# High and low part of an activation side by side, and one 512-column product for both

## The chip, the cores and the metric

The kernel runs on one core of a Trainium2 chip. The metric is the device time of one execution in microseconds: the median of three timed runs. A profiled execution of the same program has its own time and a trace; the numbers that are worked out below come from that trace.

## The reference

A trunk of two layers over 256 tokens of width 1024, all in float32. Cut to what matters:

```python
def hybrid_mixer(x, ...):
    q, k, v, z, xbc, dt_raw, g_att, g_ssm = _split(x @ w_in, IN_SPLITS)
    att = moba_attention(rope(q), rope(k), v)            # 16 heads of 64
    y_ssm = mamba2_branch(z, xbc, dt_raw, ...)           # 32 heads of 64, width 2048
    merged = (sigmoid(g_att) * (att @ w_attn_proj)       # 1024 x 1024
              + sigmoid(g_ssm) * (y_ssm @ w_ssm_proj))   # 2048 x 1024
    return merged @ w_out

def reference(x, ...):
    for i in range(DEPTH):                               # 2 layers
        x = layer_norm(ALPHA * x + hybrid_mixer(x, ...))
        x = layer_norm(ALPHA * x + square(relu(x @ w_up)) @ w_down)   # 1024 -> 4096 -> 1024
    return x
```

## The kernel before

**Precision.** Every large product is made of three. A float32 operand is split into a high part, rounded to the chip's short float32 format (`fp32r`), and a low part, what the rounding left. The sum of high times high, high times low and low times high is accumulated in one bank of PSUM. The high part is a cast on ScalarE (ACT), the low part a subtraction on VectorE (DVE).

**Weights.** They come in halves of 128 x 1024 floats, 512 KB each, 185 a layer. SyncE's queue loads a half (`load_half`, L119), ACT casts it (`high_half`, L125), DVE subtracts (`low_half`, L133). `need(L, h, s)` says in which slot a half is used: its low part is issued four slots ahead, its high part six, its load fourteen.

**Order.** The whole kernel is one list of slots, 370 a layer. A slot holds the matmuls of about 1.4 us. `at(s, f)` hangs other work in front of slot s. In each slot the order is: high casts, low parts, hung steps, loads, the slot's matmuls; every engine runs what it gets in this order, and waits where its input isn't there. `res(s)` takes the next free slot for a step that has matmuls of its own.

**Two kinds of product.** `cols` and `rows` (through `mm3`, L143 to L145) keep 128 tokens as weights of the array and move 512 columns of the weight matrix. `gemm_ct` (L407 to L409) does it the other way: a 128 x 128 tile of the weight matrix is loaded, and the 256 tokens are moved, so that the output stands with channels on partitions. One slot of `gemm_ct` does four steps of 128 rows (k), three products of 256 columns each; two slots make 128 output channels over 1024 rows.

**Who uses gemm_ct.** The input projection's state space part (`acc_x`), its gates (`acc_z`, `acc_ga`, `acc_gs`) and the step sizes (`dtp`); then the three that are touched here: the attention projection (`acc_ap`, slots B+178 on, two 256-column outputs share a bank), the state space projection (`acc_sp`, slots B+194 on, 2048 rows, four slots per output) and the up projection of the MLP in chunks 1 to 7 of 512 channels (`up`, four outputs of 128 channels per chunk, two of them in a bank). Chunk 0 of up goes through `cols` and is transposed (`hTt`, `up_turn`). Within a period of 16 slots eight slots of up alternate with eight of the down projection (`acc_d`).

**Evacuation.** `ap_evac` multiplies a full bank by the attention gate on DVE (L849). `merge` multiplies by the other gate and adds (L857, L858), then `merge_high` and `merge_low` split the result for the output projection. In the MLP `up_relu` reads a bank on ACT (L910), `up_square` squares on DVE (L914), `up_high` and `up_low` split into `hT` for the down projection.

**Banks.** Eight banks of PSUM: four with the tag `acc`, two `yav`, two `tmp`. Up's outputs are in `yav`, transposes in `tmp`. **SBUF** for activations: x as two tiles xh and xl of 128 x 8 x 256, attT and yT as pairs of tiles (high, low) of 128 x 4 x 256 (`new_T`), from the same pool of 31 tiles as the weights.

Of the kernel before, what the change touches and what calls it, by code (L numbers as in the profile page):

```python
# [64 lines left out]
def trunk(ctx: ExitStack, tc: tile.TileContext, x, xT, pos, w, pch, hp, lnp, out):  # L65
# [172 lines left out]
    def new_x(name):  # L238
        return (sb.tile([128, KD, S], F32R, name=name + "h", tag="xh", bufs=1),
                sb.tile([128, KD, S], F32R, name=name + "l", tag="xl", bufs=1))  # L240
# [71 lines left out]
    def new_T(name):  # L312
        return (u_tile(name + "h", F32R, (128, 4, S)), u_tile(name + "l", F32R, (128, 4, S)))

# [68 lines left out]
    def plan_layer(L):  # L383
# [14 lines left out]
        def gemm_ct(o, h, half, src=None, k0=None, nh=1):  # L398

            wh, wl = W[L, h]  # L400
            src = src or xsrc
# [192 lines left out]
        def ct_bank(base, h0, c0, c1, name, src, nh=1):  # L594

            g = {}

            def slot(c, half):
                if c == c0 and half == 0:
                    g["o"] = new_acc(f"acc_{name}{L}_{c}")  # L600
                o = g["o"][:, (c - c0) * S:(c - c0) * S + S]
                gemm_ct(o, h0 + nh * c + half // 2, half % 2, src, 4 * half, nh)

            for c in range(c0, c1):
                for half in range(2 * nh):
                    s = base + 2 * nh * c + half
                    if half % 2 == 0:
                        need(L, h0 + nh * c + half // 2, s)
                    slots[s] = (slot, c, half)
            return g  # L610
# [9 lines left out]
        for d, name, base, h0, n, func in ((zs, "z", B + 114, 57, 4, AF.Silu), (ga, "ga", B + 146, 73, 2, AF.Sigmoid),  # L620
                                           (gs, "gs", B + 162, 81, 2, AF.Sigmoid)):
            for b in range(n):
                banks = [ct_bank(base, h0, 4 * b + 2 * j, 4 * b + 2 * j + 2, name, None) for j in range(2)]
                at(base + 8 * b + 8, act_evac, d, b, banks, func, name)
# [59 lines left out]
        def at_out(s, g):  # L684
            if g % 2 == 0:
                attT[g // 2] = new_T(f"attT{L}{g // 2}")
            r = slice(2 * (g % 2), 2 * (g % 2) + 2)
            split_psum(s, attT[g // 2][0][:, r, :], attT[g // 2][1][:, r, :], G.pop(("av", g)))
# [120 lines left out]
        def ss_high(g):  # L809
            if g % 2 == 0:  # L810
                yT[g // 2] = new_T(f"yT{L}{g // 2}")
            k = 2 * (g % 2)
            nc.scalar.copy(out=yT[g // 2][0][:, k:k + 2, :], in_=E["y", g])

        def ss_low(g):
            k = 2 * (g % 2)
            hi, lo = (a[:, k:k + 2, :] for a in yT[g // 2])
            nc.vector.tensor_tensor(out=lo, in0=E.pop(("y", g)), in1=hi.bitcast(F32), op=OP.subtract)
# [128 lines left out]
        for c in range(1, 8):  # L947
# [176 lines left out]
```

## Time and profile before

| | |
|---|---|
| timed, median of three | 1173.37 us |
| timed, lowest and highest | 1172.96 and 1173.97 us |
| the profiled execution, its own time | 1172.3 us |
| its span, from the first to the last instruction | 1170.6 us |
| granted TensorE clock over the span | 0.997 |
| TensorE matmul (PE), busy | 1150.9 us, 8160 products |
| VectorE (DVE), busy | 864.3 us |
| ScalarE (ACT), busy | 650.7 us |
| read from HBM | 208.93 MB, 179 GB/s |

PE is the matmul engine and PEld its loading of weights, which overlaps. A row of the timeline begins with the start and the duration; successive matmuls overlap, so the distance of two starts is less than a duration. In groups, the numbers behind the first bar are the busy time and the mean duration in ns; those behind the second are the engine's idle time ahead of these instructions and what ended it. In a list of waits the numbers are the total, how often, and the longest.

### The profile page before, as it was taken

The numbers are of one execution on the slowest core, as the hardware profiler recorded it, in microseconds if no ns is written. First come the engines' busy times: TensorE is split into PE (matmuls) and PEld (weight loads), VectorE is DVE, ScalarE is ACT, GpSimd is POOL, SyncE is SP. The second block draws the span as 40 slices with busy tenths as digits, with TensorE's granted clock in tenths as the row PEclk, the third lists the DMA queues.
The fourth block names the chain that finished last, engine by engine and source line by source line (L and its number), as shares of the span: only waits on it lengthen the run. The fifth ranks groups of instructions, "written<-read, shape, count | busy, mean of one in ns | idle before, by whom it ended". The sixth has DMA issues, their size and how long they took to land.

```text
span 1170.6 us, 20414 instructions
## 1 busy us (share of the span) xinstructions
PE 1150.9 (98%) x8160; PEld 1058.4 (90%) x8160; DVE 864.3 (74%) x1553; ACT 650.7 (56%) x927; POOL 54.9 (5%) x67
## 2 busy tenths in 40 slices
PE   6999999999999999999999999999999999999996
PEld 5999888999999899989889998889999998998995
DVE  4888987799865874564689888778987668556455
ACT  5665655888734363453456656568886353444341
POOL 1000000011110100000000000000111100000000
PEclk9999999999999999999999999999999999999998
DMA  9545564544466655557336455544445656555630
GB/s 343 189 144 181 193 181 159 180 137 137 163 210 216 241 185 194 187 196 248 132 104 218 146 180 190 193 155 170 134 150 181 219 214 215 199 181 192 204 126 36
DMA packets 61263, 211.37 MB, mean 181 GB/s; under 512 B 6993, under 2 KB 7345, under 8 KB 61169
## 3 DMA queue, kind: packets, MB, share of 16 engines
q1 hardware_dynamic: 59136, 204.04, 51.2%
q0 software_dynamic: 1744, 5.51, 1.5%
q8 instruction: 64, 1.05, 0.4%
q10 hardware_dynamic: 288, 0.52, 0.1%
q14 instruction: 31, 0.25, 0.1%
HBM read 208.93 MB, written 1.11 MB: 179 GB/s over the span
## 4 chain that ended last, share of the span: by engine, by line
PE 96%; DVE 2%; DMA 1%; SPq 0%; POOL 0%; issue 0%; POOLq 0%; ACT 0%
PE acc_x L407 5%; PE acc_x L409 5%; PE acc_x L408 5%; PE acc_d L143 5%; PE acc_d L145 5%; PE acc_d L144 5%; PE up L409 5%; PE up L408 5%; PE up L407 5%; PE acc_z L407 3%; PE acc_sp L409 3%; PE acc_sp L408 3%; PE acc_sp L407 3%; PE acc_z L408 3%; PE acc_z L409 3%; PE yp L748 2%
## 5 line engine op out<-in xcount | busy, mean ns | idle before, releaser
L133 DVE TENSOR_TENSOR wlo<-raw,whi 128x1024 fp32r<-128x1024 f32 (+1 forms) x371 | 443.8, 1217 | 27.1 <-ACT whi L125 12.5
L125 ACT CAST whi<-raw 128x1024 fp32r<-128x1024 f32 (+1 forms) x371 | 375.5, 1046 | 29.2 <-PE acc_ap L408 7.6
L505 DVE SCALAR_TENSOR_TENSOR cv<-acc_x,pc,cv 128x253 f32<-128x253 f32 (+2 forms) x192 | 92.4, 481 | 18.6 <-ACT cv L501 13.9
L914 DVE TENSOR_TENSOR rl<-rl 128x512 f32<-128x512 f32 x32 | 22.1, 691 | 110.5 <-ACT rl L910 110.3
L910 ACT ACTIVATE rl<-up 128x512 f32<-128x512 f32 x28 | 16.8, 599 | 153.8 <-PE up L409 134.0
L407 PE MATMUL acc_x<-x2h,whi 128*128 128x256 f32 x256 | 74.0, 289 | 0.0
L407 PE MATMUL acc_x<-x0h,whi 128*128 128x256 f32 x256 | 73.9, 289 | 0.0
L409 PE MATMUL acc_x<-x0h,wlo 128*128 128x256 f32 x256 | 72.4, 283 | 0.0
L409 PE MATMUL acc_x<-x2h,wlo 128*128 128x256 f32 x256 | 72.4, 283 | 0.0
L408 PE MATMUL acc_x<-x0l,whi 128*128 128x256 f32 x256 | 72.4, 283 | 0.0
L408 PE MATMUL acc_x<-x2l,whi 128*128 128x256 f32 x256 | 72.4, 283 | 0.0
L501 ACT ACTIVATE cv<-acc_x,pc 128x256 f32<-128x256 f32 x64 | 36.2, 566 | 62.1 <-PE acc_x L409 59.3
L407 PE MATMUL up<-x1h,whi 128*128 128x256 f32 x224 | 63.5, 284 | 0.0
L407 PE MATMUL up<-x3h,whi 128*128 128x256 f32 x224 | 63.5, 284 | 0.0
L409 PE MATMUL up<-x3h,wlo 128*128 128x256 f32 x224 | 63.4, 283 | 0.0
L409 PE MATMUL up<-x1h,wlo 128*128 128x256 f32 x224 | 63.4, 283 | 0.0
L408 PE MATMUL up<-x1l,whi 128*128 128x256 f32 x224 | 63.4, 283 | 0.0
L408 PE MATMUL up<-x3l,whi 128*128 128x256 f32 x224 | 63.4, 283 | 0.0
L332 POOL TENSOR_TENSOR rc<-rc,mhalf 128x8 f32<-128x8 f32 x16 | 32.0, 2002 | 612.1 <-DVE nm L656 445.0
L407 PEld LDWEIGHTS acc_x<-x0h,whi 128*128 128x128 f32 x256 | 49.0, 191 | 0.3 <-issue 0.2
L407 PEld LDWEIGHTS acc_x<-x2h,whi 128*128 128x128 f32 x256 | 49.0, 191 | 0.3 <-issue 0.2
L408 PEld LDWEIGHTS acc_x<-x0l,whi 128*128 128x128 f32 x256 | 49.1, 192 | 0.0
(749 smaller groups left out, 3511.9 us busy)
## 6 DMA issues: line engine op xcount, KB each, us to landing
raw<-in_w_dram SPq DMA_DIRECT2D x369, 512.0 KB, 3.8
pb<-csd SPq DMA_DIRECT2D x32, 256.0 KB, 3.9
ln<-in_lnp_dram POOLq DMA_DIRECT2D x16, 256.0 KB, 4.9
x_tok<-in_x_dram POOLq DMA_DIRECT2D x1, 1024.0 KB, 10.9
xraw<-in_xT_dram SPq DMA_DIRECT2D x3, 256.0 KB, 7.8
raw<-in_w_dram SPq DMA_DIRECT2D x2, 256.0 KB, 3.9
out_dram<-x_tok SPq DMA_DIRECT2D x2, 256.0 KB, 2.0
out_dram<-x_tok ACTq DMA_DIRECT2D x2, 256.0 KB, 2.0
```

Of the source, the lines that this page charges most:

```text
L125: nc.scalar.copy(out=hi[:, c], in_=raws[key][:, c])
L133: nc.vector.tensor_tensor(out=lo[:, c], in0=raw[:, c], in1=W[key][:, c].bitcast(F32), op=OP.subtract)
L143: nc.tensor.matmul(o, xh, wh, start=first, stop=False)
L144: nc.tensor.matmul(o, xh, wl, start=False, stop=False)
L145: nc.tensor.matmul(o, xl, wh, start=False, stop=last)
L332: nc.gpsimd.tensor_tensor(out=dst, in0=src, in1=mhalf[:, 0:n], op=OP.pow)
L407: nc.tensor.matmul(o, a, xh[:, kk, :], start=(k == 0), stop=False)
L408: nc.tensor.matmul(o, a, xl[:, kk, :], start=False, stop=False)
L409: nc.tensor.matmul(o, b, xh[:, kk, :], start=False, stop=(k == 8 * nh - 1))
L501: nc.scalar.activation(c, o, AF.Identity, scale=pc[:, q + 3:q + 4], bias=pc[:, q + 4:q + 5])
L505: nc.vector.scalar_tensor_tensor(out=c[:, d:S], in0=o[:, 0:S - d], scalar=pc[:, q + j:q + j + 1], in1=c[:, d:S], op0=OP.mult, op1=OP.add)
L748: nc.tensor.matmul(yp[64 * i:64 * i + 64, 128 * t:256], xt[:, t, hs], e[:, i, 256 * t:256 + 128 * t], start=(t == 0), stop=(t == 1))
```

## The change

Three projections (attention, state space, up chunks 1 to 7) get a new form of `gemm_ct`, `gemm_ct2`. High and low part of the activation lie next to each other, 256 columns each, and one product of 512 columns multiplies both by the high weights. Its left half is high times high, its right half high times low. The product with the low weights, 256 columns, is accumulated onto the left half. An output of 128 channels now fills a bank of 512 columns, and its halves must be added: ACT copies the right half to SBUF (`take_right`), DVE adds the left half to it (`add_left`).

- x (`new_x`) becomes one tile of 128 x 8 x 2 x 256; attT and yT (`new_T2`) become two tiles of 128 x 2 x 2 x 256 each.
- In up the outputs take `yav` and `tmp` banks in turn, one for each 128 channels. Relu on ACT and square on DVE are replaced by the copy and the add per output, and one DVE instruction (relu and square in one) for each 512 columns.
- In the attention projection each output has its own `acc` bank; the gate multiply goes from one per 512 columns to one per 256, behind the add.
- In the state space projection the copy and the add come ahead of the gate multiply; `merge`, `merge_high` and `merge_low` of all but the last output move one slot later.
- The other projections keep `gemm_ct`, with three products of 256 columns. No load, no weight and no cast of a weight is changed.

```diff
     def new_x(name):
-        return (sb.tile([128, KD, S], F32R, name=name + "h", tag="xh", bufs=1),
-                sb.tile([128, KD, S], F32R, name=name + "l", tag="xl", bufs=1))
+        both = sb.tile([128, KD, 2, S], F32R, name=name, tag="xhl", bufs=1)
+        return both[:, :, 0, :], both[:, :, 1, :], both
...
+    def new_T2(name):
+        return [u_tile(f"{name}{i}", F32R, (128, 2, 2, S)) for i in range(2)]
...
+        def gemm_ct2(o, h, half, src, k0=None, nh=1):
+            wh, wl = W[L, h]
             k0 = 4 * half if k0 is None else k0
             for i in range(4):
                 k, c = k0 + i, (4 * half + i) * 128
-                xh, xl, kk = src(k)
+                x2, kk = src(k)
                 a, b = wh[:, c:c + 128], wl[:, c:c + 128]
-                nc.tensor.matmul(o, a, xh[:, kk, :], start=(k == 0), stop=False)
-                nc.tensor.matmul(o, a, xl[:, kk, :], start=False, stop=False)
-                nc.tensor.matmul(o, b, xh[:, kk, :], start=False, stop=(k == 8 * nh - 1))
+                last = k == 8 * nh - 1
+                left = lambda: nc.tensor.matmul(o[:, 0:S], b, x2[:, kk, 0, :], start=False, stop=False)
+                if last:
+                    left()
+                nc.tensor.matmul(o, a, x2[:, kk].rearrange("p j s -> p (j s)"), start=(k == 0), stop=last)
+                if not last:
+                    left()
+
+        def take_right(out, o):
+            nc.scalar.copy(out=out, in_=o[:, S:2 * S])
+
+        def add_left(out, o):
+            nc.vector.tensor_tensor(out=out, in0=o[:, 0:S], in1=out, op=OP.add)
...
-        def ap_evac(c, g):
-            a = ga[c // 4][:, c % 4:c % 4 + 2, :].rearrange("p k s -> p (k s)")
-            nc.vector.tensor_tensor(out=a, in0=g["o"], in1=a, op=OP.mult)
-
-        for c in range(0, 8, 2):
-            g = ct_bank(B + 178, 89, c, c + 2, "ap", lambda k: (*attT[k // 4], k % 4))
-            at(B + 178 + 2 * c + 5, ap_evac, c, g)
+        T2 = {}
+
+        def right_aside(c, g, name):
+            T2[name, c] = sb.tile([128, S], F32, name=f"{name}s{L}{c}", tag="e15", bufs=4)
+            take_right(T2[name, c], g["o"])
+
+        def ap_gate(c, g):
+            a, t = ga[c // 4][:, c % 4, :], T2.pop(("ap", c))
+            add_left(t, g["o"])
+            nc.vector.tensor_tensor(out=a, in0=t, in1=a, op=OP.mult)
+
+        for c in range(8):
+            g = ct_whole(B + 178, 89, c, "ap", lambda k: (attT[k // 4][k % 4 // 2], k % 2))
+            at(B + 178 + 2 * c + 2, right_aside, c, g, "ap")
+            at(B + 178 + 2 * c + 3, ap_gate, c, g)
...
         def merge(c, g):
-            m = gs[c // 4][:, c % 4, :]
-            nc.vector.tensor_tensor(out=m, in0=g["o"][:, 0:S], in1=m, op=OP.mult)
+            m, t = gs[c // 4][:, c % 4, :], T2.pop(("sp", c))
+            add_left(t, g["o"])
+            nc.vector.tensor_tensor(out=m, in0=t, in1=m, op=OP.mult)
...
-            g = ct_bank(B + 194, 97, c, c + 1, "sp", lambda k: (*yT[k // 4], k % 4), nh=2)
+            g = ct_whole(B + 194, 97, c, "sp", lambda k: (yT[k // 4][k % 4 // 2], k % 2), nh=2)
             r = B + 194 + 4 * c + 4
-            at(r, merge, c, g)
-            at(r + (c < 7), merge_high, c)
-            at(r + (c < 7), merge_low, c)
+            at(r, right_aside, c, g, "sp")
+            at(r + (c < 7), merge, c, g)
+            at(r + 2 * (c < 7), merge_high, c)
+            at(r + 2 * (c < 7), merge_low, c)
...
         def up_slot(c, i, half):
-            if half == 0 and i % 2 == 0:
-                ub[c, i // 2] = new_yav(f"up{L}{c}{i}")
-            o = ub[c, i // 2][:, (i % 2) * S:(i % 2) * S + S]
-            gemm_ct(o, 125 + 8 * (c - 1) + i, half, msrc)
+            if half == 0:
+                ub[c, i] = (new_tmp if i % 2 else new_yav)(f"up{L}{c}{i}")
+            gemm_ct2(ub[c, i], 125 + 8 * (c - 1) + i, half, lambda k: (X[2 * L + 1][2], k))
+
+        def up_part(c, i):
+            return hr[c][:, i // 2, (i % 2) * S:(i % 2) * S + S]
+
+        def up_right(c, i):
+            if i == 0:
+                hr[c] = u_tile(f"rl{L}{c}")
+            take_right(up_part(c, i), ub[c, i])
+
+        def up_left(c, i):
+            add_left(up_part(c, i), ub.pop((c, i)))
+
+        def up_relu_square(c, j):
+            r = hr[c][:, j, :]
+            nc.vector.scalar_tensor_tensor(out=r, in0=r, scalar=0.0, in1=r, op0=OP.max, op1=OP.mult)
...
             for j in range(2):
                 e = base + 4 + 4 * j
-                at(e, lambda c=c, j=j: up_relu(c, j, ub[c, j]))
-                at(e + 2, up_square, c, j)
+                for i in (2 * j, 2 * j + 1):
+                    at(base + 2 * i + 2, up_right, c, i)
+                    at(base + 2 * i + 3, up_left, c, i)
+                at(e + 2, up_relu_square, c, j)
                 at(e + 4, up_high, c, j)
                 at(e + 5, up_low, c, j)
```

## Rows read from the trace of the kernel before

**Rows 1.** The page: its head and the line of busy times.
```profile
span 1170.6 us, 20414 instructions
...
PE 1150.9 (98%) x8160; PEld 1058.4 (90%) x8160; DVE 864.3 (74%) x1553; ACT 650.7 (56%) x927; POOL 54.9 (5%) x67
```

**Rows 2.** Who PE waited for, longest total first; first and last of four rows.
```profile
PE acc_q00a L143 <- ACT whi L125: 6.3, 2, 6.1
...
PE lb0x L319 <- DVE x_tok L365: 0.8, 1, 0.8
```

**Rows 3.** PE groups by line and form (count, busy us, mean ns).
```profile
L407 PE MATMUL up<-x1h,whi 128*128 128x256 f32 x224 | 63.5, 284 | 0.0
...
L407 PE MATMUL acc_ap<-attT00h,whi 128*128 128x256 f32 x32 | 9.1, 283 | 0.0
...
L407 PE MATMUL acc_sp<-yT00h,whi 128*128 128x256 f32 x32 | 9.1, 283 | 0.0
...
L143 PE MATMUL acc_d<-whi,hT00h 128*128 128x512 f32 x16 | 6.2, 390 | 0.0
```

**Rows 4.** Timeline of PE where up follows down (start us, duration us).
```profile
440.16 0.39 PE L145 MATMUL acc_d<-whi,hT00l 128*128 128x512 f32 x1
440.39 0.28 PE L407 MATMUL up<-x1h,whi 128*128 128x256 f32 x1
```

**Rows 5.** Timeline of PE where down follows up.
```profile
451.66 0.28 PE L408 MATMUL up<-x1l,whi 128*128 128x256 f32 x1
451.78 0.28 PE L409 MATMUL up<-x1h,wlo 128*128 128x256 f32 x1
451.90 0.40 PE L143 MATMUL acc_d<-whi,hT01h 128*128 128x512 f32 x1
```

**Rows 6.** DVE groups by line and form.
```profile
L914 DVE TENSOR_TENSOR rl<-rl 128x512 f32<-128x512 f32 x32 | 22.1, 691 | 110.5 <-ACT rl L910 110.3
...
L857 DVE TENSOR_TENSOR gs<-acc_sp,gs 128x256 f32<-128x256 f32 x16 | 6.8, 423 | 17.9 <-PE acc_sp L409 17.9
...
L363 DVE SCALAR_TENSOR_TENSOR x_tok<-x_tok,lb0mv,ln 128x512 f32<-128x512 f32 x4 | 3.0, 744 | 0.0
```

**Rows 7.** ACT groups by line and form.
```profile
L910 ACT ACTIVATE rl<-up 128x512 f32<-128x512 f32 x28 | 16.8, 599 | 153.8 <-PE up L409 134.0 <-issue 19.8
...
L776 ACT CAST sh<-sq 128x256 fp32r<-128x256 f32 x16 | 6.5, 407 | 4.5 <-DVE sq L772 2.5 <-PE sqp L787 2.0
```

**Rows 8.** Windows: us; busy PE, PEld, DVE, ACT, POOL; PEclk, DMA share, GB/s.
```profile
311.30:336.40 25.10, 25.10 (x214) 24.51 (x213) 17.92 (x27) 12.18 (x16) 2.81 (x2) 1.00 0.52 169
336.40:382.60 46.20, 46.20 (x387) 46.20 (x387) 29.38 (x41) 17.95 (x23) 2.20 (x4) 1.00 0.66 229
...
440.40:462.80 22.40, 22.40 (x145) 20.51 (x144) 12.04 (x12) 9.82 (x12) 0.00 (x0) 1.00 0.55 190
```

**Rows 9.** Timeline of DVE at the end of the attention projection.
```profile
329.47 0.45 DVE L791 STREAM_TRANSPOSE rs<-sqp 128x256 f32<-128x256 f32 x1 [2.73 <-PE sqp L787]
...
332.79 0.45 DVE L798 STREAM_TRANSPOSE rs<-rc 128x256 f32<-128x256 f32 x1 [1.53 <-POOL rc L332]
...
336.93 0.69 DVE L818 TENSOR_TENSOR yT03l<-y,yT03h 128x512 fp32r<-128x512 f32 x1
```

**Rows 10.** Products that read yT03h (duration, then first and last start).
```profile
L407 PE MATMUL acc_sp<-yT03h,whi x32: 283/283/283, 340.8 to 382.2; 128*128 128x256 f32 x32
```

**Rows 11.** Timeline of DVE, PE where the state space projection ends.
```profile
384.91 0.43 DVE L867 TENSOR_TENSOR mT01l<-gs,mT01h 128x256 fp32r<-128x256 f32 x1 [0.47 <-ACT mT01h L863]
...
387.79 0.39 PE L145 MATMUL acc_o00a<-whi,mT01l 128*128 128x512 f32 x1
```

**Rows 12.** Timeline at the first two hTt transposes.
```profile
422.86 0.60 PE L319 MATMUL hTt<-ident,rl 128*128 128x128 f32 x4
...
423.49 0.59 ACT L305 CAST hT00h<-hTt 128x512 fp32r<-128x512 f32 x1 [3.71 <-PE hTt L319]
...
424.73 0.60 PE L319 MATMUL hTt<-ident,rl 128*128 128x128 f32 x4
```

More of the change, by code (lines that the diff above doesn't have):

```diff
@@ L396, in plan_layer, with gemm_ct @@
         xsrc = lambda k: (X[2 * L][0], X[2 * L][1], k)
-        def gemm_ct(o, h, half, src=None, k0=None, nh=1):
+        def gemm_ct(o, h, half):
             wh, wl = W[L, h]
-            src = src or xsrc
+            for i in range(4):
+                k, c = 4 * half + i, (4 * half + i) * 128
+                xh, xl, kk = xsrc(k)
+                a, b = wh[:, c:c + 128], wl[:, c:c + 128]
+                nc.tensor.matmul(o, a, xh[:, kk, :], start=(k == 0), stop=False)
+                nc.tensor.matmul(o, a, xl[:, kk, :], start=False, stop=False)
+                nc.tensor.matmul(o, b, xh[:, kk, :], start=False, stop=(k == KD - 1))
+        def gemm_ct2(o, h, half, src, k0=None, nh=1):
+            wh, wl = W[L, h]
             k0 = 4 * half if k0 is None else k0
@@ L591, in plan_layer, with ct_bank @@
                     at(res(base + 13 + late), qk_turn, which, c, 1)
-        def ct_bank(base, h0, c0, c1, name, src, nh=1):
+        def ct_bank(base, h0, c0, c1, name):
             g = {}
@@ L600, in slot, with ct_whole @@
                     g["o"] = new_acc(f"acc_{name}{L}_{c}")
-                o = g["o"][:, (c - c0) * S:(c - c0) * S + S]
-                gemm_ct(o, h0 + nh * c + half // 2, half % 2, src, 4 * half, nh)
+                gemm_ct(g["o"][:, (c - c0) * S:(c - c0) * S + S], h0 + c, half)
             for c in range(c0, c1):
[L605 to L609, printed above, removed]
+                need(L, h0 + c, base + 2 * c)
+                for half in range(2):
+                    slots[base + 2 * c + half] = (slot, c, half)
+            return g
+        def ct_whole(base, h0, c, name, src, nh=1):
+            g = {}
+            def slot(half):
+                if half == 0:
+                    g["o"] = new_acc(f"acc_{name}{L}_{c}")
+                gemm_ct2(g["o"], h0 + nh * c + half // 2, half % 2, src, 4 * half, nh)
+            for half in range(2 * nh):
+                s = base + 2 * nh * c + half
+                if half % 2 == 0:
+                    need(L, h0 + nh * c + half // 2, s)
+                slots[s] = (slot, half)
             return g
@@ L622, in plan_layer @@
             for b in range(n):
-                banks = [ct_bank(base, h0, 4 * b + 2 * j, 4 * b + 2 * j + 2, name, None) for j in range(2)]
+                banks = [ct_bank(base, h0, 4 * b + 2 * j, 4 * b + 2 * j + 2, name) for j in range(2)]
                 at(base + 8 * b + 8, act_evac, d, b, banks, func, name)
@@ L685, in at_out @@
             if g % 2 == 0:
-                attT[g // 2] = new_T(f"attT{L}{g // 2}")
-            r = slice(2 * (g % 2), 2 * (g % 2) + 2)
-            split_psum(s, attT[g // 2][0][:, r, :], attT[g // 2][1][:, r, :], G.pop(("av", g)))
+                attT[g // 2] = new_T2(f"attT{L}{g // 2}")
+            a = attT[g // 2][g % 2]
+            split_psum(s, a[:, :, 0, :], a[:, :, 1, :], G.pop(("av", g)))
         def at_pair(p):
@@ L810, in ss_high @@
             if g % 2 == 0:
-                yT[g // 2] = new_T(f"yT{L}{g // 2}")
-            k = 2 * (g % 2)
-            nc.scalar.copy(out=yT[g // 2][0][:, k:k + 2, :], in_=E["y", g])
+                yT[g // 2] = new_T2(f"yT{L}{g // 2}")
+            nc.scalar.copy(out=yT[g // 2][g % 2][:, :, 0, :], in_=E["y", g])
         def ss_low(g):
-            k = 2 * (g % 2)
-            hi, lo = (a[:, k:k + 2, :] for a in yT[g // 2])
+            a = yT[g // 2][g % 2]
+            hi, lo = a[:, :, 0, :], a[:, :, 1, :]
             nc.vector.tensor_tensor(out=lo, in0=E.pop(("y", g)), in1=hi.bitcast(F32), op=OP.subtract)
@@ L931, in up_slot @@
         def up_slot(c, i, half):
-            if half == 0 and i % 2 == 0:
-                ub[c, i // 2] = new_yav(f"up{L}{c}{i}")
-            o = ub[c, i // 2][:, (i % 2) * S:(i % 2) * S + S]
-            gemm_ct(o, 125 + 8 * (c - 1) + i, half, msrc)
+            if half == 0:
+                ub[c, i] = (new_tmp if i % 2 else new_yav)(f"up{L}{c}{i}")
[11 more added lines that the diff above has]
+            nc.vector.scalar_tensor_tensor(out=r, in0=r, scalar=0.0, in1=r, op0=OP.max, op1=OP.mult)
         def up_high(c, j):
```

## Prediction

> **What bounds the kernel now.** I read the page's busy line first: TensorE (PE) is busy for 1150.9 of 1170.6 us, and none of the other engines for more than 74% (PEld is the weight load of PE itself) [rows 1]. Busy time of pipelined matmuls can hide waits, so I looked next at what PE waited for: four rows, the first 6.3 us for weights at the very start, the last 0.8 us at the seam between the layers [rows 2]. Nowhere else does PE stand still, so the time is PE's number of products times the distance at which they follow each other. What a product costs must therefore not be read from its duration (283 ns for 256 columns, 390 ns for 512 [rows 3]), which overlaps that of the next, but from start to start in the timeline. At the place where the down projection ends and the up projection begins, a 512-column product is followed by one of 256 after 0.23 us [rows 4]; where it goes the other way, the 256-column products follow each other after 0.12 us and the first of 512 follows the last of them after 0.12 us too [rows 5]. Over a whole chunk the same comes out finer: its 22.40 us, the last window of [rows 8], hold 96 products of 256 columns and 48 of 512. The starts in the 256-column run are 120 ns apart (0.24 us for two in [rows 5]), which makes 11.52 us; the remaining 10.88 us over 48 are 226.7 ns each. So 256 more columns cost 106.7 ns, and each product, whatever its width, costs about 13.3 ns besides. That 13.3 ns is all that the change can win per product saved.
>
> **What PE gains.** For each k step of 128 rows there were three products of 256 columns (high times high, low times high, high times low): 3 x 120 = 360 ns. After it there is one of 512 (high and low side by side against the high weights) and one of 256: 226.7 + 120 = 346.7 ns. The same columns are streamed; one product fewer is issued. The gain is 13.3 ns per k step. The steps are counted from the groups: 224 for up in a layer, two groups of 32 for the attention projection (acc_ap), four groups of 32 for the state space projection (acc_sp) (one group of each in [rows 3]): 224 + 64 + 128 = 416 a layer, 832 in both. 832 x 13.3 ns = 11.1 us. All of it lies on PE and on the path that sets the end.
>
> The Trainium skill speaks against even this much: "TensorE: Matmul & The Clock Gate", section "Back-to-back issue gap", gives N / 2.4 GHz plus 2.5 ns from one matmul to the next at the full clock (the granted clock is 1.00 in [rows 8], the 2.4 GHz level). By that a step would go from 327.5 to 325.0 ns and the change would bring 2.1 us (an estimate from that page). The trace disagrees: 120 and 226.7 ns are 13.3 ns above the 106.7 and 213.3 ns that the page's first term gives, so the rows' price is used.
>
> **What ACT and DVE pay.** The two halves of a bank must now be added. For prices I take the nearest rows: a DVE add of 256 columns out of PSUM as the multiply by the gate, 0.423 us; the combined relu and square of 512 columns as the layer norm's scalar-tensor-tensor, 0.744 us, against 0.691 for the square alone [rows 6]. An ACT copy of 256 columns out of PSUM has no row; it lies between half of the relu's 0.599 us for 512 and the 0.407 us of a 256-column cast [rows 7], and I take 0.40, since fixed cost does not halve.
> Up, per chunk of 512 channels (7 a layer): ACT 4 x 0.40 - 2 x 0.599 = +0.4 us; DVE 4 x 0.423 + 2 x (0.744 - 0.691) = +1.8 us. In the 22.40 us of a chunk DVE works 12.04 and ACT 9.82 [rows 8], so DVE goes to 13.8 of about 22.0: no backlog. Their waits say the same: the relu waited 134.0 us for PE and the square 110.3 us for the relu [rows 6, 7], so both arrive early and what is added shortens waits. The copy on ACT waits for PE's last product of a pair of slots, and behind it in ACT's queue stand the high casts of weights due six slots later; behind DVE's add stand the low parts due four slots later. A slot is 12 products, 1.44 us, so four are 5.8 us against 0.8 us of added latency. Each chunk uses its four banks once; a bank is emptied three slots after its product begins and asked for again sixteen slots after it: no wait for a bank.
> Attention projection, per layer: ACT +8 x 0.40 = 3.2 us; DVE 16 x 0.423 less four gate multiplies of 0.69 (as [rows 6], 512 columns) = +4.0 us. DVE is idle for 25.10 - 17.92 = 7.2 us of this stretch, the first window of [rows 8], part of it in waits for the state space mean and for POOL's power [rows 9], into which the gates fall. This is the tightest place: the last low part of yT stands behind seven of the eight gates. It ended at 336.93 + 0.69 = 337.6 us [rows 9] and PE first touches its tile at 340.8 [rows 10], 3.2 us later. DVE's added 4.0 us find some 7 us of idle time, and PE comes there 64 x 13.3 ns = 0.9 us sooner: about 1 to 3 us of slack remain. Cost 0; without that idle time it would be up to 4.0 + 0.9 - 3.2 = 1.7 us a layer.
> State space projection, per layer: ACT +3.2 us, DVE +8 x 0.423 = 3.4 us, in the second window's 46.20 us of which DVE works 29.38 [rows 8]; it waits 17.9 us there for PE in both layers together [rows 6]. At its end the copy, the add and the old chain (multiply, add, cast, subtract) stand before the output projection. The last low part now ends at 384.91 + 0.43 = 385.3 us and PE wants it at 387.79 [rows 11]. One copy and one add more are 0.8 us: 1.6 us are left. Cost 0.
>
> **Where PE will wait.** The odd products of up take their banks from the two that the transposes also use. In each layer the second transpose of the first chunk (hTt) is issued when both are held: one by the first transpose, one by up's product of the slots just before it, whose add stands later in the program. In rows: after the start of the first transpose the cast runs from 0.63 to 1.22 us [rows 12], then ACT's copy (to 1.63) and DVE's add (to 2.1 us with the hand-overs). The second transpose came 1.87 us after the first (424.73 - 422.86 [rows 12]); one slot of four k steps lies between them, so it would come 4 x 13.3 ns sooner, at 1.82. PE waits about 0.3 us in each layer, 0.6 in all. Bounds: 0 if a bank comes free otherwise; if it waits for the first transpose's subtract, queued on DVE behind the add and 0.69 us long, 2.8 - 1.8 = 1.0 us a layer, 2.0 in all.
> At nothing I put the new shape of x, attT and yT: the same elements go through the same engines, and the projections that are not changed read rows of 256 as before. No weight load, no DMA and no queue is moved; weights are asked for about 1% sooner, and the DMA engines are busy for 0.52 to 0.66 of their time in these stretches [rows 8].
>
> **Sum.** The profiled execution took 1172.3 us (span 1170.6 and 1.7 around it), 1.1 us under the median of 1173.4. 1172.3 - 11.1 + 0.6 = 1161.8 us; against the median, 1162.9 us, a gain of 0.9%.
>
> **Rivals.**
> 1. The price per product is not saved: the 13.3 ns would belong to a change of weights in step with equal widths and turn up again, doubled, where widths alternate. Then nothing comes off and the wait at hTt stays: 1173.4 + 0.6 = 1174.0 us. Against it: 512 then 256 stands in [rows 4] at 0.23, 256 then 512 in [rows 5] at 0.12, without any surcharge. The same time comes if the wide operand is split again, so that the change does not do what it says; the down projection issues 512 columns in one product [rows 3]. Together 0.04. By the figure of "TensorE: Matmul & The Clock Gate" in the Trainium skill, above, the time would be 1173.4 - 2.1 + 0.6 = 1171.9 us, an estimate; that too is within 0.2%.
> 2. Hand-overs eat half: PE waits for banks or low parts at the seams (hTt at its upper bound 2.0; yT 1.7 a layer, 3.4): 1162.9 - 0.6 + 2.0 + 3.4 = 1167.7 us. For it: DVE is fullest there. Against it: the slacks worked out above. 0.09.
> 3. Slower: DVE becomes the bound from the attention to the state space projection. The queue is in order, every gate waits for an ACT copy, and if the waits that are idle now do not fill, DVE's 4.0 + 3.4 and ACT's 3.2 + 3.2 us a layer all push PE: 2 x 13.8 = 27.6 us of delay less 11.1, 1173.4 + 16.5 = 1189.9 us. It turns the result from 5.6 us of delay a layer on (11.1 / 2), beyond the 3.2 us by which yT is early. Against it: DVE 29.38 of 46.20 and 17.92 of 25.10. 0.04.
>
> **How the numbers follow.** The forecast, 1162.9, has 0.83. Its own range is 1162.3 (no wait at hTt) to 1164.3 (2.0 there). Rivals 1 to 3 hold 0.17. The range goes down to 1161.3, since medians of three differ by about 1 us, and up to 1167.7, which takes in rival 2. A difference under 0.2% (2.3 us) can't be told from no change: faster 0.92 (forecast and rival 2), same 0.04 (rival 1), slower 0.04 (rival 3).
>
> **What would show it.** In the changed kernel's trace: in up, 512 starts followed after 0.23 and 256 after 0.12 us, a chunk of 22.0 us instead of 22.40, the attention projection 0.9 and the state space projection 1.7 us shorter. 832 matmuls fewer. PE's waits should gain only rows at hTt, about 0.3 us each; the relu's waits on ACT turn into waits of the copies. Wrong it would be if PE waits for DVE or ACT in the projections, if the step is not near 347 ns, or if ACT's copy takes well over 0.41 us.

## The result, and the profile after

The changed kernel takes 1167.76 us (median of five; 1167.0 to 1168.84), the kernel before 1173.37 beside it (1172.96 to 1174.75): a ratio of 0.995 with a 95% interval of 0.9937 to 0.9963. It is faster, as forecast, but by 5.6 us where 10.5 were forecast, and 1167.76 lies just above the range's upper end of 1167.7.

The head and the line of busy times of the page, of the changed kernel (to be held against [rows 1]):

```profile
span 1166.0 us, 18833 instructions
...
PE 1146.7 (98%) x7328; PEld 1015.5 (87%) x7328; DVE 892.4 (77%) x1649; ACT 666.2 (57%) x987; POOL 53.1 (5%) x67
```

832 products fewer, as counted (8160 to 7328); DVE works 28 us more and ACT 16 us more. Did PE pay for that in waits? What PE waited for (total, times, longest), the whole list:

```profile
PE acc_q00a L143 <- ACT whi L125: 6.3, 1, 6.3
PE acc_q00a L144 <- DVE wlo L133: 3.0, 2, 2.3
PE lb0x L324 <- DVE x_tok L370: 0.8, 1, 0.8
```

These are the waits of [rows 2]: the start, and the seam between the layers. No wait for ACT or DVE in the three projections appears. One new row stands in the list of PE's weight loads:

```profile
PEld hTt L324 <- DVE rl L435: 0.7, 2, 0.3
```

So the missing half of the gain isn't in waits. The windows of the attention projection, the state space projection and one chunk of the MLP (columns as in [rows 8]):

```profile
312.97:337.38 24.41, 24.41 (x148) 20.86 (x147) 20.88 (x37) 13.26 (x21) 1.68 (x2) 1.00 0.57 179
337.38:382.61 45.23, 45.23 (x258) 39.27 (x256) 31.09 (x47) 21.65 (x31) 2.19 (x4) 1.00 0.73 231
440.33:462.49 22.16, 22.16 (x113) 18.82 (x112) 13.18 (x16) 10.22 (x14) 0.00 (x0) 1.00 0.61 188
```

PE is busy throughout, at a granted clock of 1.00 (the 2.4 GHz level), and each stretch became shorter by about half of what was expected. Where it went stands in the timeline of PE, at the place of [rows 4] (start, duration):

```profile
440.33 0.39 PE L427 MATMUL up<-x,whi 128*128 128x512 f32 x1
440.56 0.28 PE L424 MATMUL up<-x,wlo 128*128 128x256 f32 x1
440.67 0.40 PE L427 MATMUL up<-x,whi 128*128 128x512 f32 x1
440.91 0.28 PE L424 MATMUL up<-x,wlo 128*128 128x256 f32 x1
441.02 0.40 PE L427 MATMUL up<-x,whi 128*128 128x512 f32 x1
441.26 0.28 PE L424 MATMUL up<-x,wlo 128*128 128x256 f32 x1
441.38 0.40 PE L427 MATMUL up<-x,whi 128*128 128x512 f32 x1
441.62 0.28 PE L424 MATMUL up<-x,wlo 128*128 128x256 f32 x1
441.73 0.40 PE L427 MATMUL up<-x,whi 128*128 128x512 f32 x1
```

The first pair is the one that the forecast knew: 0.23 from the wide product to the narrow one, 0.11 to the next wide one. From the second pair on the wide product holds the next one off for 0.24 us. Four pairs take 441.73 - 440.33 = 1.40 us, and from the second on a pair takes 0.353 us on average (441.73 - 440.67 = 1.06 for three). That is 353 ns a step instead of the forecast 346.7, against 360 before.

### The profile page after: what moved, and what is told of

The parts are those of the page before. It is cut to its first block, busy times and chain, and to the rows that moved or that the text cites. A ratio compares the mean times of both kernels' runs of the same rounds, so it can differ in the third digit from the quotient of the medians.

```text
span 1166.0 us, 18833 instructions
## 1 busy us (share of the span) xinstructions
PE 1146.7 (98%) x7328; PEld 1015.5 (87%) x7328; DVE 892.4 (77%) x1649; ACT 666.2 (57%) x987; POOL 53.1 (5%) x67
## 4 chain that ended last, share of the span: by engine, by line
PE 96%; DVE 2%; DMA 1%; SPq 0%; POOL 0%; issue 0%; POOLq 0%; ACT 0%
PE up L427 9%; PE acc_x L410 5%; PE acc_x L411 5%; PE acc_x L412 5%; PE acc_sp L427 5%; PE acc_d L143 5%; PE acc_d L144 5%; PE acc_d L145 5%; PE up L424 5%; PE acc_z L410 3%; PE acc_z L411 3%; PE acc_z L412 3%; PE acc_sp L424 3%; PE acc_ap L427 3%; PE yp L787 2%; PE acc_ga L410 1%
## 5 line engine op out<-in xcount | busy, mean ns | idle before, releaser
L427 PE MATMUL up<-x,whi 128*128 128x512 f32 x448 | 156.6, 398 | 0.0
L410 PE MATMUL acc_x<-x,whi 128*128 128x256 f32 x512 | 148.1, 289 | 0.0
L412 PE MATMUL acc_x<-x,wlo 128*128 128x256 f32 x512 | 145.0, 283 | 0.0
L411 PE MATMUL acc_x<-x,whi 128*128 128x256 f32 x512 | 144.9, 283 | 0.0
L424 PE MATMUL up<-x,wlo 128*128 128x256 f32 x448 | 116.7, 281 | 0.0
L410 PEld LDWEIGHTS acc_x<-x,whi 128*128 128x128 f32 x512 | 98.1, 192 | 0.6 <-issue 0.4
L411 PEld LDWEIGHTS acc_x<-x,whi 128*128 128x128 f32 x512 | 98.2, 192 | 0.0
L412 PEld LDWEIGHTS acc_x<-x,wlo 128*128 128x128 f32 x512 | 98.1, 192 | 0.0
L427 PEld LDWEIGHTS up<-x,whi 128*128 128x128 f32 x448 | 81.5, 188 | 15.6
L427 PE MATMUL acc_sp<-yT,whi 128*128 128x512 f32 x256 | 89.5, 399 | 0.0
L424 PEld LDWEIGHTS up<-x,wlo 128*128 128x128 f32 x448 | 84.7, 189 | 5.0
L410 PE MATMUL acc_z<-x,whi 128*128 128x256 f32 x256 | 74.8, 292 | 0.0
L411 PE MATMUL acc_z<-x,whi 128*128 128x256 f32 x256 | 72.4, 283 | 0.0
```

What stands on the lines that cost most here:

```text
L424: left = lambda: nc.tensor.matmul(o[:, 0:S], b, x2[:, kk, 0, :], start=False, stop=False)
L427: nc.tensor.matmul(o, a, x2[:, kk].rearrange("p j s -> p (j s)"), start=(k == 0), stop=last)
```

## Experiments

Four theories for the 6.7 ns a step that are missing:
- **A**: a stream in which wide (512) and narrow (256) products take turns is slower than runs of one width; the price goes with the changes of width.
- **B**: the narrow product pays because it adds to columns that the product just before it wrote.
- **C**: the copies, the adds or the new layout of the activations slow PE down.
- **D**: a wide product is dearer in these projections, whatever stands beside it.

The stages, in us from the start of PE's first product of one to that of the next (layer 0). The two rows on MLP count from the first product of chunk 1 of up (the tile `up`) to the first `acc_x` product of the next layer (layer 0) and to the end (layer 1); chunk 0 of up, which is not changed, therefore stands in the row of the output projection, and the next layer's first products (queries, step sizes) in that of the MLP. A step in ns is the state space stage over its 128 steps. In the changed kernel the last step of each output issues its narrow product first, so that there, and only there, two of one width meet. In the last row, the first product of `acc_x` near the beginning of the span is taken off, because it lies at 25.80 to 28.25 us in these executions, and differs for one program too (28.25 and 26.89 for the changed kernel).

| | before | after | e1 | e2 | e3 | e4 | e6 | e7 | e9 |
|---|---|---|---|---|---|---|---|---|---|
| equal widths in a row | 3 narrow | 1 | 8 | 2 | 3 narrow | 1 | 16 | all wide | 2 |
| attention projection | 24.92 | 24.41 | 24.22 | 24.21 | 24.92 | 24.41 | 24.18 | 30.97 | 24.21 |
| state space projection | 46.08 | 45.23 | 44.69 | 44.59 | 46.08 | 45.23 | 44.53 | 58.03 | 44.59 |
| a step, ns | 360.0 | 353.4 | 349.1 | 348.4 | 360.0 | 353.4 | 347.9 | 453.4 | 348.4 |
| output projection | 34.55 | 34.53 | 34.52 | 34.52 | 34.57 | 34.57 | 36.02 | 34.55 | 34.54 |
| MLP, layer 0 | 185.25 | 183.62 | 182.92 | 182.79 | 185.45 | 183.61 | 182.47 | 206.12 | 182.53 |
| MLP, layer 1 | 178.05 | 176.39 | 175.73 | 175.55 | 178.25 | 176.40 | 175.64 | 198.93 | 175.34 |
| span less its start | 1143.78 | 1137.75 | 1134.88 | 1134.38 | 1144.24 | 1137.79 | 1136.94 | 1221.48 | 1133.91 |

### Eight of one width in a row (e1_runs4)

The same products in another order: four wide, four narrow in one slot, four narrow, four wide in the next.

```diff
-            for i in range(4):
...
-                if last:
-                    left()
-                nc.tensor.matmul(o, a, x2[:, kk].rearrange("p j s -> p (j s)"), start=(k == 0), stop=last)
-                if not last:
-                    left()
+            def wide(i):
...
+            def left(i):
...
+            order = [(wide, i) for i in range(4)], [(left, i) for i in range(4)]
+            for f, i in (order[0] + order[1] if half == 0 else order[1] + order[0]):
+                f(i)
```

> Only the order of the products is changed: in each slot of the three projections the four 512-column products stand together and so do the four of 256 (the second slot begins with the narrow ones, so that widths change once in eight products). Theory A, changes of width cost: in the changed kernel a 512 is followed after 236 ns and a 256 after 117 ns, 353 ns a step where 346.7 was forecast; with two changes a step that is 3.2 ns a change. Here there are 0.25 changes a step, so about 347.5 ns a step: 832 x 5.5 = 4.6 us less than the changed kernel, 1163.2 us. Theory C, the added work on ACT and DVE slows the products: nothing changes, 353 ns and 1167.8 us.

Measured: 1164.2 us (1162.75 to 1164.37), ratio 0.9924 (0.9911 to 0.9936). The timeline of PE in e1, where eight products of one width come in one row (the duration is that of all eight):

```profile
442.49 2.00 PE L422 MATMUL up<-x,whi 128*128 128x512 f32 x8
444.33 1.11 PE L428 MATMUL up<-x,wlo 128*128 128x256 f32 x8
445.28 0.40 PE L422 MATMUL up<-x,whi 128*128 128x512 f32 x1
```

Eight steps take 445.28 - 442.49 = 2.79 us, 349 ns each; A, as put down, expected 347.5. Nothing but the order is different from the changed kernel, so most of the missing time (4.3 of 6.7 ns a step) does belong to the order (A). C, which expected no difference, does not explain it. By single starts, the wide products behind narrow ones are followed by the next product after 233, 236, 228, 233, 231 ns and only then after 227; the narrow ones behind wide ones after 113 ns, then 119, then 120. So a change of width isn't paid once: it takes some five wide products until the distance is that of [rows 4], which costs about 27 ns, and the first two narrow ones give back 8.

### Two of one width in a row (e2_runs2)

```diff
+            for f, i in ((wide, 0), (left, 0), (left, 1), (wide, 1), (wide, 2), (left, 2), (left, 3), (wide, 3)):
+                f(i)
```

> The same eight products of a slot in the order wide, narrow, narrow, wide, wide, narrow, narrow, wide: one change of width a step in place of two. Theory A: half of the surcharge goes, 353 to about 350 ns a step, 832 x 3.2 = 2.7 us less than the changed kernel, 1165.1 us. Theory C: 1167.8 us as the changed kernel.

Measured: 1164.07 us (1163.56 to 1164.36), ratio 0.9926 (0.9914 to 0.9938). The timeline of PE in e2:

```profile
442.21 0.63 PE L422 MATMUL up<-x,whi 128*128 128x512 f32 x2
442.68 0.39 PE L428 MATMUL up<-x,wlo 128*128 128x256 f32 x2
442.91 0.62 PE L422 MATMUL up<-x,whi 128*128 128x512 f32 x2
```

Two steps take 442.91 - 442.21 = 0.70 us, 350 ns each by these rows; the state space stage gives 348.4. With half the changes of width three quarters of the surcharge are gone (6.7 to 1.7 ns a step), where A expected half; with an eighth of the changes, in e1, a little less is gone (6.7 to 2.4). A price per change, the form in which A was put down, is wrong. Over 346.7 ns a step, one round from wide to narrow and back costs, by the state space stage, 6.7 ns when every product changes (353.4), 2 x 1.7 = 3.4 in runs of two, 8 x 2.4 = 19 in runs of eight, and (e6, below) 16 x 1.2 = 19 in runs of sixteen. Strict alternation is the worst by the step, long runs pay the most by the round. The single starts show where it lies: in e2 the wide products are followed after 233, 236, 233 and 231 ns and the narrow ones after 116, 112, 113 and 119, so that the narrow ones give back most of what the wide ones cost over 227 and 120; in the changed kernel the wide ones take 232 to 241 and the narrow ones 113 to 120.

### Three narrow products on the new layout (e3_narrow)

All copies, adds and tiles of the changed kernel, but the wide product is issued as two of 256 columns.

```diff
+                nc.tensor.matmul(o[:, 0:S], a, x2[:, kk, 0, :], start=(k == 0), stop=False)
+                nc.tensor.matmul(o[:, 0:S], b, x2[:, kk, 0, :], start=False, stop=False)
+                nc.tensor.matmul(o[:, S:2 * S], a, x2[:, kk, 1, :], start=False, stop=last)
```

> The wide product is taken back: three products of 256 columns a step as before, but into the two halves of a bank, with the layout, the banks, the copies and the adds of the changed kernel. Theory A: 360 ns a step as before, so the time is that of the kernel before plus the wait at hTt of 0.3 us a layer: 1174.0 us. Theory C: the steps are longer than 360 ns, by 6 ns and more, and the time is 1173.4 + 0.6 + 832 x 6.4 ns = 1179.3 us.

Measured: 1173.47 us, ratio 1.0004 (0.9995 to 1.0013). The timeline of PE in e3:

```profile
441.47 0.28 PE L426 MATMUL up<-x,whi 128*128 128x256 f32 x1
441.59 0.28 PE L424 MATMUL up<-x,whi 128*128 128x256 f32 x1
441.71 0.28 PE L425 MATMUL up<-x,wlo 128*128 128x256 f32 x1
441.83 0.28 PE L426 MATMUL up<-x,whi 128*128 128x256 f32 x1
```

0.12 us apart, as before. The attention and state space stages are those of the kernel before to 0.01 us. What the evacuation and the layout cost is nearly all in the MLP, 0.40 of the 0.46 us that the span loses, 0.20 a layer: the wait at `hTt`, 0.2 us a layer in this run's list of waits. C falls as a cause of the loss in the steps, and the forecast's "cost 0" for ACT and DVE is shown, at 360 ns a step; at 353 the changed kernel's list of waits shows it.

### The narrow product on the other half (e4_right)

The product with the low weights is added onto the right half, columns 256 to 511 of the bank, instead of the left.

```diff
-                left = lambda: nc.tensor.matmul(o[:, 0:S], b, x2[:, kk, 0, :], start=False, stop=False)
+                left = lambda: nc.tensor.matmul(o[:, S:2 * S], b, x2[:, kk, 0, :], start=False, stop=False)
```

> The narrow product is accumulated onto the right half of the bank, not the left; the sum of the halves is the same. The wide product writes its right half last, so the narrow one meets columns written about 107 ns earlier, not 213. Theory A: no difference, 353 ns a step and 1167.8 us. Theory B, the array or the bank waits for columns that were just written: the step changes, by some ns up to the 107 ns of a half, so over 1170 us, or, if the next wide product was the one that waited for the left half, down to 347 ns and 1163 us.

Measured: 1165.44 us (1165.23 to 1167.03), ratio 0.9941 (0.9928 to 0.9955). The timeline of PE in e4:

```profile
439.68 0.40 PE L427 MATMUL up<-x,whi 128*128 128x512 f32 x1
439.92 0.28 PE L424 MATMUL up<-x,wlo 128*128 128x256 f32 x1
440.04 0.40 PE L427 MATMUL up<-x,whi 128*128 128x512 f32 x1
440.28 0.40 PE L424 MATMUL up<-x,wlo 128*128 128x256 f32 x2
```

Again 0.24 and 0.12, and every stage agrees with the changed kernel to 0.04 us. In the profiled execution the span is 2.4 us shorter, and all of it is the start (25.80 us to the first `acc_x` against 28.25). Which of the two halves is written plays no part. The narrow product touches columns that the wide one has just written in both cases, though; that this by itself costs nothing is shown by e7, where every product does so, and by e3, where one of three does.

### The changed kernel once more (e5_changed_again)

No edit: to see how far its time is repeated in another session.

> The changed kernel as it is, beside the others of this call. It and the variant with the narrow product on the right half had equal times in every stretch from the first acc_x product on, and yet lay 2.3 us apart (1167.8 and 1165.4); the difference stood ahead of the first acc_x product, which started at 28.25 us in the one profile and at 25.80 in the other. If that start varies from session to session, this run lies near 1165.5 to 1166.5 us; if it belongs to the program, at 1167.8 us again.

Measured: 1167.01 us (1165.62 to 1167.77), ratio 0.9949 (0.9936 to 0.9961). The stages are those of the first execution, the span less its start 1137.72 against 1137.75. Its start lies between the two (26.89 us), and so does its time: the scatter of about a microsecond lies in the start, and varies for one program.

### Sixteen of one width in a row (e6_runs16)

Eight wide products of one output, eight of the next, then the narrow ones of both, over four slots (in the state space projection, of the two halves of one output's 2048 rows); in the attention projection and the MLP the evacuation of the first of the two comes a slot later.

```diff
+        def wides(o, h, src, k0=0):
+            wh, wl = W[L, h]
+            for i in range(8):
...
+        def lefts(o, h, src, k0=0, last=True):
...
+        def ct_pair(base, h0, c, name, src):
...
+                (wides if j < 2 else lefts)(g["o"], h0 + c + j % 2, src)
...
+                    at(base + 4 * j + 3 + i % 2, up_right, c, i)
+                    at(base + 4 * j + 4 + i % 2, up_left, c, i)
```

> The order of the products again, now in runs of sixteen: two outputs of the attention and up projections (or the two halves of 2048 rows in the state space projection) get their sixteen wide products first and then their sixteen narrow ones; copies and adds of the first of two outputs move one slot later. Theory A, in its second form: products of one width settle at 120 or 227 ns, and the first few after a change of width do not; a round trip of widths cost 19 ns with runs of eight (349.1 ns a step). With runs of sixteen a step costs 346.7 + 19 / 16 = 347.9 ns, 832 x 1.2 = 1.0 us less than with runs of eight: 1163.2 us. Theory D, a wide product costs some ns more here wherever it stands, because of what it reads: 349 ns as with runs of eight, 1164.2 us.

Measured: 1166.55 us (1166.44 to 1166.78), ratio 0.9947 (0.9935 to 0.996). The steps are as A expects: 347.9 ns, and in the timeline of PE in e6 sixteen steps take 445.89 - 440.35 = 5.54 us, 346 ns each, in the first round after a long run of wide products:

```profile
440.35 3.79 PE L418 MATMUL up<-x,whi 128*128 128x512 f32 x16
443.98 2.08 PE L425 MATMUL up<-x,wlo 128*128 128x256 f32 x16
445.89 0.40 PE L418 MATMUL up<-x,whi 128*128 128x512 f32 x1
```

But the output projection became 1.5 us longer in each layer. The last two slots of the state space projection now hold narrow products alone and are short, and the chain behind them (copy, add, two more on DVE, cast, subtract) no longer ends in time: the copy ends at 383.16 us, but the add starts at 384.98, behind the low parts of the output before and of a half of weights in DVE's queue. Two of the waits that PE has now, from its list in e6 (two alike stand for layer 1):

```profile
PE la0x L324 <- DVE x_tok L370: 0.5, 1, 0.5
...
PE acc_o00a L143 <- ACT mT01h L924: 0.5, 1, 0.5
```

They account for 1.0 of the 1.5 us. By starts each costs more: in the timeline of PE the product that waits comes 0.85 us after the one before it (385.96 to 386.81, and 402.38 to 403.23), where 0.23 is usual, and the next few are late by another 0.06 to 0.13, together about 1.4 us. The time forecast by A, 1163.2 us, was missed by 3.4 us, and 3.0 of them are these two layers' seams: what the order gained was lost there.

### The same with another bank for up's second output (e8_runs16_bank)

```diff
-                ub[c, ii] = (new_tmp if ii % 2 else new_yav)(f"up{L}{c}{ii}")
+                ub[c, ii] = (new_acc if (c, ii) == (1, 1) else new_tmp if ii % 2 else new_yav)(f"up{L}{c}{ii}")
```

> As the runs of sixteen, and the second output of chunk 1 of up takes a bank with the tag acc, so that the second hTt transpose finds a free one. The trace of the changed kernel showed the weight load of hTt waiting 0.3 us a layer for DVE's add, as forecast. This wait goes: 0.6 us less than the runs of sixteen, 1162.6 us. If something else ends last there, no change.

Measured: 1166.21 us (1164.44 to 1167.23), ratio 0.9944 (0.993 to 0.9957); the span less its start 1136.98 against 1136.94 in e6. No effect: e6 has no wait at `hTt` that could go. Its copy and add come as long after the first transpose as in the changed kernel (1.12 and 1.53 us), but the slot between the two transposes holds eight wide products, so that the second is issued 2.29 us after the first (422.96 and 425.25), when the bank is free. The expectation had carried the wait over from the changed kernel without looking for its row.

### All products wide (e7_all_wide)

The product with the low weights takes 512 columns too, so that low times low is added to the result as well.

```diff
-                left = lambda: nc.tensor.matmul(o[:, 0:S], b, x2[:, kk, 0, :], start=False, stop=False)
+                left = lambda: nc.tensor.matmul(o, b, x2[:, kk].rearrange("p j s -> p (j s)"), start=False, stop=False)
```

> The narrow product is made wide: the low weights multiply high and low part too (the sum gains the product of the two low parts). All products of the three projections then have 512 columns. Theory A: with one width only, each costs 226.7 ns as in the down projection, 453.3 a step: 832 x (453.3 - 353.1) = 83.4 us over the changed kernel, about 1250 us. Theory D: 231 to 236 ns each, 462 to 472 a step, 1257 to 1266 us.

Measured: 1250.12 us, ratio 1.0659 (1.064 to 1.0679). The timeline of PE in e7:

```profile
519.65 0.39 PE L427 MATMUL up<-x,whi 128*128 128x512 f32 x1
519.87 0.39 PE L424 MATMUL up<-x,wlo 128*128 128x512 f32 x1
520.10 0.39 PE L427 MATMUL up<-x,whi 128*128 128x512 f32 x1
520.33 0.39 PE L424 MATMUL up<-x,wlo 128*128 128x512 f32 x1
```

0.227 us apart (0.68 for three), the price of [rows 4] and of the down projection. So a wide product costs here what it costs elsewhere, and D falls. Here each product also adds to columns that the one before it wrote, at no surcharge: with e3 and e4, B falls. With e3 this closes the case between the widths: three narrow ones at 120 ns each, two wide ones at 227 ns each, both in the same layout, with high and low weights taking turns; only where both widths stand in one stream does the step miss its sum.

### Two in a row, and the wait at hTt taken away (e9_runs2_bank)

e2, with an `acc` bank for the second output of the first chunk, so that both banks of the transposes are free when the second transpose comes.

```diff
-                ub[c, i] = (new_tmp if i % 2 else new_yav)(f"up{L}{c}{i}")
+                ub[c, i] = (new_acc if (c, i) == (1, 1) else new_tmp if i % 2 else new_yav)(f"up{L}{c}{i}")
```

> Runs of two (wide, narrow, narrow, wide) with a bank of the tag acc for the second output of chunk 1 of up. In the runs of sixteen this bank changed nothing, because PE did not wait at hTt there; in the runs of two the weight load of hTt does wait, 0.3 us a layer. If that wait is the bank's, the time from the first acc_x product to the end falls from 1134.38 us by 0.5 to 0.7 us, and the whole by as much: about 1163.3 us where the kernel before takes 1172.9. If the wait only moves, 1164 us.

Measured: 1163.28 us (1161.7 to 1164.75), ratio 0.9919 (0.9906 to 0.9933). The span less its start fell by 0.47 us, at the lower end of what was expected (0.5 to 0.7). The row at `hTt` is gone from the list of waits, and the MLP is shorter than in e2 by 0.26 us in layer 0 and 0.21 in layer 1. In the timed medians 0.5 us can't be told from nothing; in the stages it can. This version beats the kernel before and the changed one: its interval lies below those of the two runs of the changed kernel (0.9937 to 0.9963, 0.9936 to 0.9961).

## Why the prediction was half right

**What bounds the kernel: right.** PE's stream sets the time, and the gain came off that stream alone. All 832 products went, no stretch of the projections gained a wait.

**The price per product: the step that failed, in size.** "So 256 more columns cost 106.7 ns, and each product, whatever its width, costs about 13.3 ns besides." For streams of one width this is exact: 120 ns in e3 and 227 ns in e7. The forecast carried it over to alternating widths on the strength of [rows 4] and [rows 5], one change of width each, behind a long run of one width. Those two rows are true, and the changed kernel repeats them in its first pair (0.23 and 0.11). But the second pair already takes 0.35 us, and those that follow 0.353 on average. A single change does not show what a stream of changes costs; the trace of before had no such stream, and the forecast gave this term no bound of its own.

A sign did stand in it, one row further. The timeline of PE of the kernel before, behind the last of [rows 5] (451.90):

```profile
452.13 0.40 PE L144 MATMUL acc_d<-wlo,hT01h 128*128 128x512 f32 x1
452.37 0.39 PE L145 MATMUL acc_d<-whi,hT01l 128*128 128x512 f32 x1
...
453.06 0.39 PE L145 MATMUL acc_d<-whi,hT01l 128*128 128x512 f32 x1
...
453.74 0.39 PE L145 MATMUL acc_d<-whi,hT01l 128*128 128x512 f32 x1
```

The first five distances behind the change take 453.06 - 451.90 = 1.16 us, 232 ns each; only the next three take 0.68, 227 each. So the change of width had its surcharge there too, as in e1, once a chunk. The chunk's sum hid it by luck: from its first product to that of the next chunk it takes 462.81 - 440.39 = 22.42 us, not the 22.40 of the window, and the 0.02 left out are just what the change costs net.

The miss by stages, from the table: the attention projection gained 0.51 us a layer of the forecast 0.85 (64 x 13.3 ns), the state space projection 0.85 of 1.70, the MLP (with `hTt`) 1.65 of 2.98 - 0.3 = 2.7. Together 3.0 a layer of 5.2, or 6.0 us of 10.5, and 1143.78 - 1137.75 = 6.03 us is what the span lost behind its start. The median fell by 5.6.

**Rival 1 was the nearest in mechanism, and priced as all or nothing.** It said that the price per product would "turn up again, doubled, where widths alternate", and gave 1174.0. Half of it turned up again: 6.7 of 13.3 ns. What the forecast held against it, "without any surcharge", rested on the same two rows. Between "none" and "all" there was no case in the forecast; such a case, half the price, would have given 1162.9 + 5.5 = 1168.4 us, 0.6 above what came. Rival 2 gave 1167.7 for another reason, lost time at the seams, and that did not happen: the time near its figure is no support for it.

**What ACT and DVE pay: right.** The groups of the new work (busy us, mean ns; then the idle time ahead of it and who ended it):

```profile
L432 ACT COPY rl<-up 128x256 f32<-128x256 f32 x56 | 20.9, 372 | 143.6 <-PE up L427 143.6
...
L435 DVE TENSOR_TENSOR rl<-up,rl 128x256 f32<-128x256 f32 x56 | 23.8, 425 | 118.4 <-ACT rl L432 118.4
...
L997 DVE SCALAR_TENSOR_TENSOR rl<-rl 128x512 f32<-128x512 f32 x28 | 19.2, 685 | 0.0
```

The prices held. The copy took 0.372 (taken at 0.40, bounds 0.30 and 0.407), the add 0.425 (0.423). The relu and square in one took 0.685, as much as the square alone in [rows 6], not the 0.744 of the row that was taken: that row also reads two more operands, those of the layer norm. Copies still wait for PE and adds for the copies, so the work is hidden, and e3 shows it as a whole: it costs nothing but `hTt`. Only the sum of DVE's work was too high: its busy time rose by 28 us, where the forecast's terms make 2 x (12.6 + 4.0 + 3.4) = 40. The instructions are as many as counted (96 more); some that follow each other directly overlap in the trace (below, the add from 424.29 to 424.71 and the subtract from 424.64), which adding up durations counts twice. That this is all of the difference is not shown.

**The tight places held.** The last low part of yT and the last of mT01 against the product that needs it, in the timeline of DVE and PE:

```profile
338.16 0.68 DVE L856 TENSOR_TENSOR yT<-y,yT 128x512 fp32r<-128x512 f32 x1
...
386.15 0.43 DVE L914 TENSOR_TENSOR mT01l<-gs,mT01h 128x256 fp32r<-128x256 f32 x1 [0.47 <-ACT mT01h L910]
...
387.83 0.39 PE L145 MATMUL acc_o00a<-whi,mT01l 128*128 128x512 f32 x1
```

yT is done at 338.84; the state space projection begins at 337.38 and comes to step 12 of 16, from which the forecast counted, twelve times 353 ns later, at 341.6: 2.8 us of slack, forecast 1 to 3. (In the new layout the tile written last holds only steps 14 and 15, so the real slack is two steps more, 3.5 us.) mT01l is done at 386.58, wanted at 387.83: 1.25 us, forecast 1.6. e6 shows what happens when a seam is given less: waits, at once.

**The wait at hTt: right.** Timeline of PE, ACT, DVE and weight loads at the place of [rows 12]:

```profile
422.76 0.60 PE L324 MATMUL hTt<-ident,rl 128*128 128x128 f32 x4
...
423.88 0.38 ACT L432 COPY rl<-up 128x256 f32<-128x256 f32 x1
...
424.29 0.42 DVE L435 TENSOR_TENSOR rl<-up,rl 128x256 f32<-128x256 f32 x1 [1.59 <-ACT rl L432]
424.64 0.68 DVE L310 TENSOR_TENSOR hT00l<-hTt,hT00h 128x512 fp32r<-128x512 f32 x1
424.77 0.42 PEld L324 LDWEIGHTS hTt<-ident,rl 128*128 128x128 f32 x4 [0.33 <-DVE rl L435]
```

The second transpose follows the add that ends at 424.71, not the subtract that ends at 425.32: 0.33 us, forecast 0.3 with a bound of 1.0. e9 takes the bank away from up and gets 0.26 and 0.21 us back.

**The Trainium skill's figure.** By the formula in "TensorE: Matmul & The Clock Gate", section "Back-to-back issue gap", in the Trainium skill, the change would have brought 2.1 us on PE (an estimate). Measured is 6.0. In streams of one width the traces give 120 and 227 ns where this formula gives 109.2 and 215.8 for 256 and 512 columns. The same section of the Trainium skill says that the formula is that of an isolated matmul, which the forecast left out, and gives about 131 ns at 512 columns for a stream of weight loads and matmuls; the 227 ns of e7 lie far above that too. On streams of mixed width, which decided here, it gives no figure.

**What stays open.** That mixed widths are the cause is shown by e1, e2, e3 and e7. Why it takes some five wide products after a narrow one to reach 227 ns, and why two in a row cost less by the round than eight, was not settled: no view tells what the engine does between two starts.

## What to carry to other kernels

Price a new stream of instructions from a row with the same repetition: a single change between two long runs is not the price of a stream of changes. If the trace has no such stream, follow the rows behind a single change until the distance is steady again, and put a case between "all saved" and "none saved" into the forecast. Where a kernel needs products of 512 and 256 columns, issue two or more of each in a row, and leave the last group of a stage long enough to hide the evacuation behind it.

## What the runs showed of the hardware that was not expected

Products of 512 and 256 columns that take turns follow each other after 232 to 241 and 113 to 120 ns, 353 ns a pair (granted clock 1.00), though each alone keeps 227 (e7) and 120 ns (e3). Behind a run of narrow products it takes about five wide ones, at some 232 ns each, before they follow each other after 227 (e1, e6, and the kernel before). In runs of two, eight and sixteen a pair comes to 348.4, 349.1 and 347.9 ns in the state space projection, 44.59, 44.69 and 44.53 us for 128 pairs. So pairing up two is already worth 0.64 us of that stage's 45.23; runs of eight are worth 0.54, runs of sixteen 0.70.
